# Six tile pairs of an MLP up projection as seven products of halves

## The chip, the cores and the metric

The program runs on one core of one Trainium2 chip. The metric is the device time of one execution in microseconds (us). Three timed runs of the kernel before gave 926.32, 927.02 and 927.61 us, with the median 927.02.

## The reference

One layer of a hybrid decoder, followed by a gated MLP, on 512 tokens (SEQ) of 1024 features (D_MODEL), in fp32. The mixers in front of the MLP stay as they are. What matters here is the MLP, whose hidden width D_FF is 3072, with a gate half and a value half:

```python
x = x + merged @ w_out[l]
h2 = rms_norm(x, norm_ffn[l])
up = causal_dwconv(h2 @ w_up[l], ffn_conv_w[l], ffn_conv_b[l])
gate_h, val_h = jnp.split(up, 2, axis=-1)
x = x + (jax.nn.gelu(gate_h, approximate=True) * val_h) @ w_down[l]
```

`w_up` is 1024 x 6144 and `w_down` 3072 x 1024. `causal_dwconv` has width 3: each output channel is a weighted sum of the same channel at a token and at the two tokens ahead of it, plus a bias. A root mean square norm with a gain ends the function.

## The kernel before

**Numbers.** TensorE works on fp32 data as two fp32r parts: `split` (L97, L98) rounds a tile to its high part on ScalarE and subtracts that from the tile on VectorE (or on GpSimd, where it is given as `eng`) for the low part. `mm3` (L104) makes a product from three passes, high by high, high by low and low by high, that add up in one PSUM bank. A product over 128 features is so three matmuls.

**The up projection.** The 3072 channels of each half are 24 tiles of 128. A *tile pair* is a gate tile and the value tile of the same channels. Normed x2 (`h2`, channels on partitions, tokens along the free axis) stays in SBUF as eight blocks of 128 features, high and low. One *unit* makes one tile: `fetch` (L166) loads a 128x1024 weight tile (512 KB) on SyncE's queue into one of three `raw` buffers, `split` makes its two parts, and `channel_major` issues 8 x 3 = 24 matmuls of 128x512 into one of five `mm` banks. `up_evac` then reads the bank: ScalarE scales by one convolution weight and adds the bias (L1162), and VectorE adds the two shifted terms in two steps (L1164). After the value tile `up_done` applies Gelu (L1174, ScalarE) and multiplies the halves (L1175, VectorE). The first three units are special: they multiply tokens 0 to 255 first and tokens 256 to 511 later, while the second half of the tokens is being normed and transposed (`norm2_flip`).

**Seven products.** The helper `seven`, used before this stage for two projections and after it for the first 20 tiles of the down projection (`down_fast`), makes a product of 2 x 2 blocks from seven block products rather than eight. Its blocks carry names: a1, a2, c1, c2, b1, b2, b3. Its weights are sums of blocks, and those are made in the transfer: a block is loaded by SyncE (L294), and then GpSimd issues transfers that add other blocks to the buffer where it lies (L299, *accumulating fetches*). A buffer to which a fetch adds must have been split before, since the sum replaces what was there.

**What sets the order.** The program is a list of *units*, which hold TensorE work, and *steps*. Each unit may name other work with a lead: `emit` places it that many units ahead (a weight tile is fetched and split two units ahead, AHEAD). `run` appends units and steps one after the other, and `blend` mixes the units of the up projection with those of `down_fast` evenly. The order of each engine's instructions comes from this list and a scheduler that has the tile dependencies. Each engine works through its own list in order, and an instruction that waits holds back those behind it. Activations, sums and fetched blocks share a pool of 51 slots of 128x512 fp32 (`fslot`, `rslot`). PSUM has five banks for `bank` and three for `sbank`.

At the end of the program `blend` runs tile pairs 12 to 19 with the down projection of tiles 0 to 11, and pairs 20 to 23 with that of tiles 12 to 19. Tile pairs 0 to 11 are run by themselves by `weave`, at about 537 to 656 us of the span: 24 units.

Of the kernel before, what the change touches and what calls it, by code (L numbers as in the profile page):

```python
# [8 lines left out]
F32 = mybir.dt.float32  # L9
# [4 lines left out]
AF = mybir.ActivationFunctionType  # L14
ALU = mybir.AluOpType
# [3 lines left out]
P = 128  # L19
# [38 lines left out]
def trunk(ctx: ExitStack, tc: tile.TileContext, x, xT, mem, memT, par, wdecay, wch, wv, wg, wmk,  # L58
# [20 lines left out]
    def rslot(shape=(P, S)):  # L79
        return apool.tile(list(shape), F32R, tag="s", name=nm("r"))  # L80
# [1021 lines left out]
    def down_units(wd, acts, after, between=None, left=None, nk=4):  # L1102

        def evac(t, ps, c):

            with tc.issue_after(queue.pop()) if queue else ExitStack():
                add = nc.vector.tensor_tensor(out=x2[t][c], in0=x2[t][c], in1=ps, op=ALU.add)
# [10 lines left out]
        lhs = lambda k, t: tuple(a[:, t * P:(t + 1) * P] for a in acts[k])  # L1118
# [32 lines left out]
    wo = down_units(wout, mr, norm2, norm2_flip)  # L1151
    step(lambda: residual(0))
    weave(wo[:4], [])
    step(lambda: residual(1))
# [15 lines left out]
    def up_done(ps, i, half, keep):  # L1170
        uph[half] = up_evac(ps, NF * half + i)
        if half:
            a, b = uph[0], uph[1]
            nc.scalar.activation(a, a, AF.Gelu_apprx_tanh)  # L1174
            nc.vector.tensor_tensor(out=a, in0=a, in1=b, op=ALU.mult)  # L1175
            keep(a)

    def up_units(tiles, keep, early=0):

# [19 lines left out]

    kept = {}

    def down_fast(at, np, acts, first, last):
# [3 lines left out]
        def sums(p):  # L1208

            A = {}  # L1210
            for j in range(2):
                ev, od = acts[2 * (2 * p + j)], acts[2 * (2 * p + j) + 1]
# [88 lines left out]
        else:  # L1301
            right()

    acts = [[] for _ in range(3)]

    def halves(a):
        r = (rslot(), rslot())
        split(*r, a)
        acts[2].append(r)
# [3 lines left out]
    blend(up_units(range(20, NF), halves), down_fast(3, 2, acts[1], False, True))  # L1313
    step(lambda: gain_rows(gfin))
    weave(down_units(wdown2, acts[2], final, None, final_left, 2), [])

    emit()

# [90 lines left out]
```

## Time and profile before

| | |
|---|---|
| median of three runs | 927.02 us |
| profiled execution | 928.05 us |
| its span, first to last instruction | 926.3 us |
| mean granted TensorE clock | 0.998 |
| busy: TensorE matmul, weight load | 99%, 84% |
| busy: VectorE, ScalarE, GpSimd | 68%, 54%, 12% |
| mean DMA rate | 126 GB/s |
| TensorE busy at 537 to 656 us (up projection alone) | 118.75 of 119.00 us |
| VectorE, ScalarE, GpSimd busy there | 65.93, 46.67, 0.00 us |
| DMA engines busy there | 0.28 |

Engines are PE (TensorE matmul), PEld (its weight load), DVE (VectorE), ACT (ScalarE), POOL (GpSimd) and SP (SyncE). L104 is line 104 of the kernel. In a list of single instructions the first two numbers are the start in the span and the duration in us, and brackets hold the idle time ahead and what ended it. In a group, `x48 | 37.5, 781 | 35.9` says 48 instructions, 37.5 us busy, 781 ns each, and 35.9 us of idle time ahead of them. In the table of stretches come the stretch and its length, then busy time (and instructions) of PE, PEld, DVE, ACT and POOL, then the granted clock, the busy share of the DMA engines and GB/s.

### The profile page before, as it was taken

Reading aid. Unit: us, or ns where it says so; the run is one execution under the profiler, and the core shown is the slowest. Engines: PE = TensorE matmul, PEld = TensorE weight load, DVE = VectorE, ACT = ScalarE, POOL = GpSimd, SP = SyncE. Lnnn points to the kernel's source line nnn. Section 1 sums busy time; section 2 is a strip of 40 time slices with the busy share of each in tenths; the row PEclk is TensorE's granted clock in tenths of the full one; section 3 lists DMA queues with packets and bytes.
Section 4 is the critical chain, followed back from the end, with each engine's and each line's share of the span. In section 5 each row is a group of like instructions: output and inputs, shape, how many; then the busy total and the mean of one; then the engine's idle time right before and its main releaser. Section 6 shows DMA issues by size and latency. Waiting matters only on the chain.

```text
span 926.3 us, 12066 instructions
## 1 busy us (share of the span) xinstructions
PE 914.6 (99%) x4390; PEld 776.4 (84%) x4390; DVE 631.8 (68%) x1104; ACT 498.1 (54%) x810; POOL 106.7 (12%) x144
## 2 busy tenths in 40 slices
PE   9999999999999999999999999999999999999996
PEld 7899888888889998888888798888888888888885
DVE  6997755665688567747776665555586666598765
ACT  6765655585855468484534334434445445445544
POOL 0010000000233430330000000000010140013102
PEclk9999999999999999999999999999999999999999
DMA  7446223213468783321157302234555594356622
GB/s 241 142 137 215 91 87 100 89 44 117 116 162 181 175 207 119 113 86 52 52 165 249 103 24 69 91 93 129 142 114 137 137 231 111 114 136 177 142 69 91
DMA packets 45994, 116.93 MB, mean 126 GB/s; under 512 B 5568, under 2 KB 13424, under 8 KB 45936
## 3 DMA queue, kind: packets, MB, share of 16 engines
q1 hardware_dynamic: 33920, 94.99, 31.9%
q0 software_dynamic: 11872, 20.92, 12.7%
q8 instruction: 34, 0.56, 0.2%
q10 hardware_dynamic: 144, 0.26, 0.1%
q14 instruction: 24, 0.20, 0.1%
HBM read 111.69 MB, written 3.67 MB: 125 GB/s over the span
## 4 chain that ended last, share of the span: by engine, by line
PE 86%; DVE 5%; DMA 4%; ACT 2%; issue 2%; SPq 0%; POOL 0%; DVEq 0%; ACTq 0%; POOLq 0%
PE mm L104 80%; DMA f<-in_wv 2%; PE mm L436 2%; PE sm L104 2%; DMA raw<-in_wup 2%; DVE wlo L98 2%; DVE r L98 1%; ACT r L97 1%; DVE f L392 0%; PE sm L996 0%; DMA raw<-in_wch 0%; ACT whi L97 0%; PE sm L983 0%; PE sm L1010 0%; DVE f L810 0%
## 5 line engine op out<-in xcount | busy, mean ns | idle before, releaser
L98 DVE TENSOR_TENSOR wlo<-raw,whi 128x1024 fp32r<-128x1024 f32 (+3 forms) x154 | 172.1, 1121 | 139.3 <-PE mm L104 71.6
L97 ACT ACTIVATE whi<-raw 128x1024 fp32r<-128x1024 f32 (+3 forms) x154 | 148.2, 968 | 173.6 <-PE mm L104 138.1
L104 PE MATMUL mm<-whi,r 128*128 128x512 f32 (+2 forms) x568 | 171.5, 372 | 0.0
L104 PE MATMUL mm<-h2l,whi 128*128 128x512 f32 x360 | 140.1, 389 | 0.0
L104 PE MATMUL mm<-h2h,whi 128*128 128x512 f32 x360 | 139.9, 389 | 0.0
L104 PEld LDWEIGHTS mm<-whi,r 128*128 128x128 f32 x568 | 105.6, 188 | 15.7 <-ACT r L97 0.3
L104 PE MATMUL mm<-hh,whi 128*128 128x512 f32 x288 | 113.4, 394 | 0.0
L104 PE MATMUL mm<-hl,whi 128*128 128x512 f32 x288 | 112.7, 391 | 0.0
L104 PE MATMUL mm<-wlo,r 128*128 128x512 f32 (+2 forms) x284 | 105.7, 372 | 0.5 <-DVE wlo L98 0.5
L104 PE MATMUL mm<-r,whi 128*128 128x512 f32 (+1 forms) x432 | 94.2, 367 | 0.0
L104 PE MATMUL mm<-h2h,wlo 128*128 128x512 f32 x360 | 88.9, 389 | 0.0
L104 PEld LDWEIGHTS mm<-r,whi 128*128 128x128 f32 x432 | 75.2, 189 | 13.1
L98 DVE TENSOR_TENSOR wlo<-f,whi 128x512 fp32r<-128x512 f32 (+2 forms) x90 | 53.7, 630 | 43.5 <-ACT whi L97 29.6
L299 POOL DMA_DIRECT2D f<-in_wdown x40 | 35.1, 1023 | 412.3 <-DMA f<-in_wdown 268.9
L97 ACT ACTIVATE whi<-f 128x512 fp32r<-128x512 f32 (+2 forms) x90 | 48.0, 579 | 59.9 <-PE mm L104 45.9
L104 PEld LDWEIGHTS mm<-h2h,wlo 128*128 128x128 f32 x360 | 67.6, 188 | 14.0
L104 PEld LDWEIGHTS mm<-h2l,whi 128*128 128x128 f32 x360 | 67.6, 188 | 14.0
L104 PEld LDWEIGHTS mm<-h2h,whi 128*128 128x128 f32 x360 | 67.5, 188 | 14.0
L1164 DVE SCALAR_TENSOR_TENSOR f<-mm,prm,f 128x511 f32<-128x511 f32 x96 | 71.4, 744 | 6.9 <-ACT f L1162 6.1
L104 PE MATMUL mm<-hh,wlo 128*128 128x512 f32 x288 | 71.4, 390 | 0.0
L104 PEld LDWEIGHTS mm<-hh,wlo 128*128 128x128 f32 x288 | 54.0, 188 | 11.2
L104 PEld LDWEIGHTS mm<-hh,whi 128*128 128x128 f32 x288 | 54.1, 188 | 10.8
(245 smaller groups left out, 1341.1 us busy)
## 6 DMA issues: line engine op xcount, KB each, us to landing
raw<-in_wup SPq DMA_DIRECT2D x48, 512.0 KB, 3.5
raw<-in_wch SPq DMA_DIRECT2D x39, 512.0 KB, 3.4
f<-in_wdown POOLq DMA_DIRECT2D x40, 256.0 KB, 5.9
raw<-in_wbr SPq DMA_DIRECT2D x24, 384.0 KB, 3.1
raw<-in_wdown SPq DMA_DIRECT2D x14, 512.0 KB, 3.5
f<-in_wdown SPq DMA_DIRECT2D x20, 256.0 KB, 4.4
raw<-in_wout SPq DMA_DIRECT2D x8, 512.0 KB, 3.6
f<-in_wv POOLq DMA_DIRECT2D x16, 200.0 KB, 5.7
```

The source lines that it names most:

```text
L97: nc.scalar.activation(hi, src, AF.Copy)
L98: return (eng or nc.vector).tensor_tensor(out=lo, in0=src, in1=hi.bitcast(F32), op=ALU.subtract)
L104: nc.tensor.matmul(ps, lhsT=l, rhs=r, start=first and i == 0, stop=last and i == len(seq) - 1, skip_group_check=more)
L299: nc.gpsimd.dma_start(raw[to, p][j], src(q, p)[:, j, :], accum_op=ALU.add)
L436: nc.tensor.matmul(ps[u], lhsT=w(a, u, k), rhs=xs["r"][k][j], start=k == 0 and i < n, stop=k == KD - 1 and i >= len(seq) - n)
L1164: nc.vector.scalar_tensor_tensor(out=a[:, j:], in0=ps[:, :S - j], scalar=col(C_FCW + 48 * (2 - j) + f), in1=a[:, j:], op0=ALU.mult, op1=AL ...
```

## The change

Six of the first twelve tile pairs (3, 4, 6, 7, 9 and 10) are made by `up_fast`, as seven products of halves; pairs 0, 1, 2, 5, 8 and 11 stay as they were. Gate and value tile make the two columns of the weight matrix (B11 and B21 the first and second 512 features of the gate tile, B12 and B22 those of the value tile), and the halves of the tokens make two rows of normed x2. Each of the seven products has 4 feature blocks of three matmuls each, 256 tokens wide: 12 matmuls of 128x256. a1, b1, b2 and b3 add up in one `mm` bank, c1 and c2 in one `sm` bank, a2 has another; after a1, c1, c2 and b3 ScalarE copies the bank to SBUF (L1263), and after a2, b1 and b2 VectorE adds or subtracts it. `up_evac` then works from SBUF, and `up_mix` is the old end of `up_done`.

The weight sums come from accumulating fetches (L1246): the buffer of B11 serves a1, then B12 is added for c1, then B22 for b1, then B21 for b3, and each split is followed by the fetch for the next use. B12 in a buffer of its own gets B22 added for b2. GpSimd makes the low parts of a2, c2 and b2. The sums of normed x2 (`h2_sums`) are sixteen GpSimd operations, eight for each half of the feature blocks, once for all six pairs; their splits are made with `h2_ready`. Each fast pair runs beside one ordinary unit: b1 of the pair before, a1, the unit, b2 of the pair before, c1, a2, b3 of the pair before, c2. `blend` starts with two units less, and the activations are kept in a dictionary by tile number rather than in three lists.

```diff
+    def h2_sums(p):
+        tt, f = nc.gpsimd.tensor_tensor, {}
+        for r in range(2):
+            for c in range(2):
+                at = slice(4 * c + 2 * p, 4 * c + 2 * p + 2), slice(r * HT, (r + 1) * HT)
+                f[r, c] = fslot((P, 2, HT))
+                tt(out=f[r, c], in0=h2["h"][(slice(None), *at)].bitcast(F32), in1=h2["l"][(slice(None), *at)].bitcast(F32),
+                   op=ALU.add)
+        tt(out=f[1, 1], in0=f[1, 0], in1=f[1, 1], op=ALU.subtract)
+        tt(out=f[1, 0], in0=f[0, 0], in1=f[1, 0], op=ALU.subtract)
+        tt(out=f[0, 0], in0=f[1, 1], in1=f[0, 0], op=ALU.subtract)
+        tt(out=f[0, 1], in0=f[0, 1], in1=f[0, 0], op=ALU.add)
...
+    def h2_ready(key, p):
+        f, h2s[key, p] = h2s[key, p], (rslot((P, 2, HT)), rslot((P, 2, HT)))
+        split(*h2s[key, p], f)
...
+    def up_fast(i, keep):
+
+        src = lambda q: wup[NF * (int(q[2]) - 1) + i][:, HB * (int(q[1]) - 1):HB * int(q[1])]
+        raw, w, st = {}, {}, {}
+
+        def load(q):
+            raw[q] = fslot()
+            loads.append(nc.sync.dma_start(raw[q], src(q)))
+
+        def ready(key, q, more=None):
+            w[key] = rslot(), rslot()
+            split(*w[key], raw[q], nc.gpsimd if key in ("a2", "c2", "b2") else None)
+            if more:
+                add(q, more)
+
+        def add(q, more):
+            nc.gpsimd.dma_start(raw[q], src(more), accum_op=ALU.add)
+
+        def run(key):
+            if key == "a1":
+                st["x"], st["o"] = bank((P, HT)), (fslot(), fslot())
+            elif key in ("a2", "c1"):
+                st[key] = sbank((P, HT))
+            ps = st["c1" if key[0] == "c" else "a2" if key == "a2" else "x"]
...
+            if key in ("a1", "c1", "c2", "b3"):
+                o = {"a1": g[:, one], "c1": v[:, two], "c2": v[:, one], "b3": g[:, two]}[key]
+                nc.scalar.activation(o, ps, AF.Copy)
+            elif key == "a2":
+                tt(out=g[:, one], in0=g[:, one], in1=ps, op=ALU.add)
+            else:
+                o = v[:, one if key == "b1" else two]
+                tt(out=o, in0=o, in1=ps, op=ALU.subtract)
+            if key == "b3":
+                up_mix(*(up_evac(a, NF * half + i) for half, a in enumerate((g, v))), i, keep)
+
+        pre = {
+            "a1": [(8, lambda: load("B11")), (3, lambda: ready("a1", "B11", "B12"))],
+            "a2": [(6, lambda: load("B21")), (3, lambda: ready("a2", "B21"))],
+            "c1": [(2, lambda: ready("c1", "B11", "B22"))],
+            "c2": [(6, lambda: load("B22")), (3, lambda: ready("c2", "B22"))],
+            "b1": [(2, lambda: ready("b1", "B11", "B21"))],
+            "b2": [(9, lambda: load("B12")), (6, lambda: add("B12", "B22")), (3, lambda: ready("b2", "B12"))],
+            "b3": [(2, lambda: ready("b3", "B11"))],
+        }
+        return {key: (p, lambda key=key: run(key)) for key, p in pre.items()}
...
-    weave(up_units(range(12), acts[0].append, 3), [])
-    blend(up_units(range(12, 20), acts[1].append), down_fast(0, 3, acts[0], True, False))
...
+    us = up_units((0, 1, 2, 5, 8, 11), whole, 3)
+    run(*us[:3], [lambda: h2_sums(0)], us[3], [lambda: h2_sums(1)], us[4], us[5],
+        [lambda k=k: h2_ready(k, 0) for k in ("c1", "c2", "b1", "b2")])
+
+    ahead = None
+    for i, u in zip((3, 4, 6, 7, 9, 10), us[6:]):
+        f = up_fast(i, whole)
+        run([ahead["b1"]] if ahead else [], [f["a1"]], u)
+        if not ahead:
+            run([lambda k=k: h2_ready(k, 1) for k in ("c1", "c2", "b1", "b2")])
+        run([ahead["b2"]] if ahead else [], [f["c1"], f["a2"]], [ahead["b3"]] if ahead else [], [f["c2"]])
+        ahead = f
+    us = up_units(range(12, 20), whole)
+    run([ahead["b1"]], us[0], [ahead["b2"]], us[1], [ahead["b3"]])
+    blend(us[2:], down_fast(0, 3, group(0), True, False))
```

**ScalarE at the first fast pair.** Before, in the middle of the up projection, ScalarE's list alternates bank read-outs (L1162), splits of whole weight tiles (`whi`) and a Gelu every second unit:

```order
L1162 ACTIVATE f_1078_5410<-mm_1077_5385,prm_76 128x512
L97 ACTIVATE whi_1090_5490<-raw_1089_5488 128x1024
L1162 ACTIVATE f_1083_5447<-mm_1082_5422,prm_76 128x512
L1174 ACTIVATE f_1083_5447<-f_1083_5447 128x512
L97 ACTIVATE whi_1095_5525<-raw_1094_5523 128x1024
L1162 ACTIVATE f_1088_5482<-mm_1087_5457,prm_76 128x512
```

In the changed program, the list in the first fast pair from the copy of a1 (`mm_1103_5474`) on; `f_1080_5371` to `f_1079_5369` are sums of normed x2 and `sm_1118_5540` is the bank of c1:

```order
L1263 ACTIVATE f_1104_5475<-mm_1103_5474 128x256
L97 ACTIVATE r_1106_5490<-f_1081_5377 128x512
L1162 ACTIVATE f_1109_5519<-mm_1108_5494,prm_76 128x512
L97 ACTIVATE r_1110_5523<-f_1080_5371 128x512
L97 ACTIVATE r_1112_5527<-f_1078_5367 128x512
L97 ACTIVATE r_1114_5531<-f_1077_5365 128x512
L1176 ACTIVATE f_1109_5519<-f_1109_5519 128x512
L97 ACTIVATE r_1116_5535<-f_1079_5369 128x512
L1263 ACTIVATE f_1105_5476<-sm_1118_5540 128x256
L97 ACTIVATE r_1119_5554<-f_1002_4860 128x512
```

The copy of c1, for which c2 waits since it adds to the same bank, now stands behind the ordinary unit's read-out, its Gelu and four splits of sums.

**GpSimd in the loop of the pairs.** Before, GpSimd's list has nothing for the up projection: it goes from clearing buffers in an earlier stage to the accumulating fetches of the down projection.

```order
L985 MEMSET f_793_3988 128x512
L985 MEMSET f_795_3996 128x512
L299 DMA f_1147_5889<-in_wdown 128x512
L299 DMA f_1148_5890<-in_wdown 128x512
L299 DMA f_1159_5965<-in_wdown 128x512
```

In the changed program, from the third fetch into the second pair's B11 buffer (`f_1082_5379`, for b3) to the first fetch into the fourth pair's (`f_1161_5801`); `f_1131_5618` is the third pair's, and `f_1169_5828` holds its sum for b2:

```order
L1246 DMA f_1082_5379<-in_wup 128x512
L1246 DMA f_1131_5618<-in_wup 128x512
L98 TENSOR_TENSOR r_1159_5783<-f_1139_5645,r_1158_5782 128x512
L98 TENSOR_TENSOR r_1168_5825<-f_1154_5761,r_1167_5824 128x512
L1246 DMA f_1131_5618<-in_wup 128x512
L1246 DMA f_1169_5828<-in_wup 128x512
L98 TENSOR_TENSOR r_1175_5877<-f_1160_5799,r_1174_5876 128x512
L1246 DMA f_1131_5618<-in_wup 128x512
L1246 DMA f_1161_5801<-in_wup 128x512
```

The fetches of two neighbouring pairs follow each other, with the subtractions of b2, a2 and c2 between them, and an issue that waits for a split holds back what stands behind it.

**SyncE's loads.** Before, SyncE's list in this stage has whole tiles only (`raw`, 512 KB). In the changed program a whole tile for the ordinary unit is followed by four blocks of 256 KB for fast pairs:

```order
L166 DMA raw_1287_6578<-in_wup 128x1024
L1237 DMA f_1154_5761<-in_wup 128x512
L1237 DMA f_1160_5799<-in_wup 128x512
L1237 DMA f_1161_5801<-in_wup 128x512
L1237 DMA f_1169_5828<-in_wup 128x512
L166 DMA raw_1302_6662<-in_wup 128x1024
```

The order tells that the four blocks stand behind the whole tile, not when they land.

More of the change, by code (lines that the diff above doesn't have):

```diff
@@ L1172, in up_done, with up_mix @@
         if half:
[L1173 to L1176, printed above, removed]
+            up_mix(uph[0], uph[1], i, keep)
+    def up_mix(a, b, i, keep):
+        nc.scalar.activation(a, a, AF.Gelu_apprx_tanh)
+        nc.vector.tensor_tensor(out=a, in0=a, in1=b, op=ALU.mult)
+        keep(i, a)
     def up_units(tiles, keep, early=0):
@@ L1302, in final, with whole, halves @@
             right()
[L1304 to L1309, printed above, removed]
-    weave(up_units(range(12), acts[0].append, 3), [])
-    blend(up_units(range(12, 20), acts[1].append), down_fast(0, 3, acts[0], True, False))
-    blend(up_units(range(20, NF), halves), down_fast(3, 2, acts[1], False, True))
+    acts = {}
+    def whole(i, a):
+        acts[i] = a
+    def halves(i, a):
+        acts[i] = rslot(), rslot()
+        split(*acts[i], a)
+    group = lambda first: lambda k: acts[first + k]
+    us = up_units((0, 1, 2, 5, 8, 11), whole, 3)
[12 more added lines that the diff above has]
+    blend(us[2:], down_fast(0, 3, group(0), True, False))
+    blend(up_units(range(20, NF), halves), down_fast(3, 2, group(12), False, True))
     step(lambda: gain_rows(gfin))
-    weave(down_units(wdown2, acts[2], final, None, final_left, 2), [])
+    weave(down_units(wdown2, group(20), final, None, final_left, 2), [])
     emit()
```

19 lines of the change are left out of this document (16 added, 3 removed).

## The prediction

> **What bounds the kernel now.** First the head of the page and its chain of waits, then the stretches of the up projection, then the order of time on ScalarE there.
>
> ```profile
> span 926.3 us, 12066 instructions
> PE 914.6 (99%) x4390; PEld 776.4 (84%) x4390; DVE 631.8 (68%) x1104; ACT 498.1 (54%) x810; POOL 106.7 (12%) x144
> PE 86%; DVE 5%; DMA 4%; ACT 2%; issue 2%; SPq 0%; POOL 0%; DVEq 0%; ACTq 0%; POOLq 0%
> core 0: us, PE busy (x) PEld busy (x) DVE busy (x) ACT busy (x) POOL busy (x), PEclk, DMA share, GB/s
> 560.00:575.00 15.00, 15.00 (x68) 12.43 (x67) 7.99 (x11) 6.68 (x8) 0.00 (x0) 1.00 0.20 70
> ```
> ```profile
> 568.32 0.78 ACT L1162 ACTIVATE f<-mm,prm 128x512 f32<-128x512 f32 x1 [0.75 <-PE mm L104]
> ...
> 571.95 1.06 ACT L97 ACTIVATE whi<-raw 128x1024 fp32r<-128x1024 f32 x1 [0.17 <-PE mm L104]
> 573.76 0.78 ACT L1162 ACTIVATE f<-mm,prm 128x512 f32<-128x512 f32 x1 [0.75 <-PE mm L104]
> ```
>
> TensorE is busy 99% of the span, and in the up stage it never pauses (15.00 of 15.00) while ScalarE waits for it before every read-out. So a removed matmul is worth its pitch, and any pause that the change brings is paid in full. The read-outs stand 5.44 us apart: one unit of 24 matmuls.
>
> **The products.** A busy time cannot price a matmul, since neighbours overlap. Starts can: two stretches of 24 in a row, 512 and 256 wide.
>
> ```profile
> 22.76 3.79 PE L104 MATMUL mm<-r,whi 128*128 128x512 f32 x16
> 26.39 1.98 PE L104 MATMUL mm<-r,wlo 128*128 128x512 f32 x8
> 28.20 3.79 PE L104 MATMUL mm<-r,whi 128*128 128x512 f32 x16
> ...
> 47.13 2.08 PE L104 MATMUL mm<-r,whi 128*128 128x256 f32 x16
> 49.05 1.12 PE L104 MATMUL mm<-r,wlo 128*128 128x256 f32 x8
> 50.01 2.08 PE L104 MATMUL mm<-r,whi 128*128 128x256 f32 x16
> ```
>
> 24 of 512 take 28.20 - 22.76 = 5.44 us (0.2267 each), 24 of 256 take 2.88 (0.120). Removed: 6 pairs x 2 tiles x 24 = 288 wide ones, 65.3 us. Added: 6 x 7 products x 12 = 504 half-wide ones, 60.5 us. So an eighth fewer columns gives **-4.8 us**, not an eighth of 65.3: 8.2 by columns, less 504 x 0.0067 for the narrower form.
> The Trainium skill, "TensorE: Matmul & The Clock Gate", section "Back-to-back issue gap", has N/2.4 + 2.5 ns: 215.8 and 109.2 ns. By it the sum would be 62.2 - 55.0, a gain of 7.1 us; the rows stand 11 ns above it at both widths, and they decide.
>
> **What the other engines get.** One fast pair and the ordinary unit beside it fill 84 x 0.120 + 5.44 = 15.5 us of TensorE.
>
> ```profile
> L97 ACT ACTIVATE r<-f 128x256 fp32r<-128x256 f32 x54 | 19.0, 405 | 0.0
> L97 ACT ACTIVATE r<-f 128x512 fp32r<-128x512 f32 x28 | 16.8, 620 | 3.3 <-DVE f L1175 3.3
> L1162 ACT ACTIVATE f<-mm,prm 128x512 f32<-128x512 f32 x48 | 37.5, 781 | 35.9 <-PE mm L104 35.9
> L1174 ACT ACTIVATE f<-f 128x512 f32<-128x512 f32 x24 | 15.0, 625 | 23.9 <-DVE f L1164 23.9
> ...
> L98 DVE TENSOR_TENSOR wlo<-raw,whi 128x1024 fp32r<-128x1024 f32 x106 | 131.2, 1238 | 117.4 <-PE mm L104 63.6 <-ACT whi L97 52.8 <-issue 0.8
> L1164 DVE SCALAR_TENSOR_TENSOR f<-mm,prm,f 128x510 f32<-128x510 f32 x48 | 35.7, 745 | 0.8
> L98 DVE TENSOR_TENSOR r<-f,r 128x256 fp32r<-128x256 f32 x54 | 21.5, 416 | 0.7 <-ACT r L97 0.7
> L98 DVE TENSOR_TENSOR r<-f,r 128x512 fp32r<-128x512 f32 x28 | 18.9, 684 | 0.8 <-ACT r L97 0.7
> ...
> L1275 POOL TENSOR_TENSOR f<-m,f 128x512 f32<-128x512 f32 x4 | 5.2, 1295 | 40.3 <-DVE m L1107 40.2
> ```
>
> ScalarE, by these means: 7 weight splits x 0.62, 4 bank copies x 0.41, 2 read-outs x 0.78, one Gelu 0.63, and 2.2 for the ordinary unit: 10.3 us. VectorE: 4 x 0.68, 3 x 0.42, 4 x 0.75, one product 0.69, 3.1 for the unit: 10.7 us. GpSimd: 3 subtractions x 1.30 = 3.9, and four issues of fetches, about one microsecond each by the rows further down. None reaches 15.5, so no engine becomes the bound: 0 us, under a cover of 4.8 us or more per pair. What can cost is order and latency.
>
> **First fast pair.** Product c2 adds into c1's bank and must wait for ScalarE's copy of c1. In ScalarE's list that copy stands behind a read-out, a Gelu that needs two VectorE steps, and splits of the sums. If the unit of tile 2 ends at 573.6 (its read-out row above), a1 ends at 575.0, the ordinary unit at 580.5, c1 and a2 (24 matmuls) at 583.4. ScalarE: about 0.7 left over from earlier splits, read-out 0.78, then VectorE 0.75 + 0.68 + 0.75, Gelu 0.63, split 0.62, copy 0.41: 5.3 us, so 585.8 and with handovers 585.9. TensorE waits **+2.5 us**, once. Ends: 1.7 without that backlog, 3.8 with one GpSimd operation (1.30) in VectorE's way. Later pairs have 2.9 us of other products between c1 and c2, and no such Gelu in front.
>
> **The chain of the fetches.** All of a1, c1, b1, b3 share one buffer, into which three fetches add; ScalarE splits a1 of the next pair only after b1 of this one. So the pairs hang together in a loop: b1 split, add, c1 split, add, next b1 split. The landings:
>
> ```profile
> L299 POOL DMA_DIRECT2D f<-in_wdown x1: 921/921/921, 662.1 to 662.1; - x1
> DMA to landing us min/median/max: 4.1/4.1/4.1
> ...
> L299 POOL DMA_DIRECT2D f<-in_wdown x2: 857/1000/1142, 672.7 to 673.3; - x2
> DMA to landing us min/median/max: 4.1/4.8/5.5
> ...
> L299 POOL DMA_DIRECT2D f<-in_wdown x1: 863/863/863, 757.0 to 757.0; - x1
> DMA to landing us min/median/max: 6.0/6.0/6.0
> ```
> ```profile
> 662.00:667.00 5.00, 5.00 (x24) 4.14 (x23) 4.78 (x10) 1.82 (x2) 1.80 (x2) 1.00 0.35 52
> 672.00:678.00 6.00, 6.00 (x28) 4.99 (x27) 6.00 (x14) 3.02 (x6) 1.75 (x2) 1.00 0.54 85
> 757.00:764.00 7.00, 7.00 (x33) 5.79 (x32) 6.40 (x10) 2.52 (x4) 3.79 (x6) 1.00 0.98 240
> ```
>
> One alone lands after 4.1 us where DMA is 0.35 busy, and the leading one of two after 4.1 at 0.54, but one after 6.0 at 0.98; of two issued together the second lands at 673.3 + 5.5, that is 6.1 after the first issue. An issue holds GpSimd for 0.86 to 1.14, and how the two elementwise engines meet is seen once in the trace, around 385 to 390 (VectorE, then GpSimd):
>
> ```profile
> 384.75 0.67 DVE L963 TENSOR_TENSOR f<-f,f 96x512 f32<-96x512 f32 x1
> ...
> 387.66 1.21 DVE L98 TENSOR_TENSOR wlo<-raw,whi 128x1024 fp32r<-128x1024 f32 x1
> ...
> 389.40 1.78 DVE L963 TENSOR_TENSOR f<-f,f 96x512 f32<-96x512 f32 x1
> ```
> ```profile
> 385.50 2.22 POOL L965 TENSOR_TENSOR f<-f,f 96x512 f32<-96x512 f32 x1 [1.90 <-DVE f L963]
> 387.69 2.94 POOL L966 TENSOR_TENSOR f<-f,f 96x512 f32<-96x512 f32 x1
> ```
>
> The loop, from the landing before b1: split 0.62 + 0.68; b3's add goes out, the next pair's first add behind it lands 6.1 later; splits of c1 and a2 1.24, GpSimd's subtraction for a2 1.30, which stands before the next issue; then a landing of 4.1 to 6.0; and some 0.6 for six handovers (estimate, 0.1 each, from the 0.08 between VectorE's end at 385.42 and GpSimd's start at 385.50 in these rows). That is 10.5 plus the last landing: 14.6 to 16.5 us against the 15.5 of TensorE.
> How much the first step has to spare: the second pair's a1 starts at 585.9 + 2.9 (c2 and b1 of the first) = 588.8, and its b1 14.1 later at 602.9, so its fetch has to land by 602.2. a1 of that pair is split by 587.5, its first add lands near 593.1, and the second goes out 2.7 us later, at 595.9: it may take 6.3 us.
> Just then SyncE, released by the split of an ordinary unit, sends 512 KB and three or four loads of 256 KB in a burst. So I take 5.5 for this landing, nearer to the busy row: a loop of 16.0, 0.55 late at each of four steps (second to sixth pair), less 0.7 spare: **+1.5 us**. Ends: 0 (landing 4.1) and 3.9 (landing 6.0: four steps of 1.05, spare 0.3).
>
> **The sums of normed x2.** Sixteen GpSimd operations that the trace does not have.
>
> ```profile
> 548.46 1.29 DVE L98 TENSOR_TENSOR h2l<-sm,h2h 128x512 fp32r<-128x512 f32 x2 [1.99 <-ACT h2h L97]
> ...
> 560.10 0.74 DVE L1164 SCALAR_TENSOR_TENSOR f<-mm,prm,f 128x510 f32<-128x510 f32 x1
> ```
>
> Six of the first eight start when normed x2 is whole (549.8); then comes an accumulating fetch that waits for the first weight split on VectorE (560.84 + 0.68 = 561.5); the other eight end at 561.5 + 0.87 + 8 x 1.30 = 572.8, wanted at 581.9. Cost 0; the cover is 9 us.
>
> **The rest.** The loads and splits of the ordinary units stand further ahead than before: 0. Loads for the down projection come later, with over a unit (5.44) in hand: 0; without that cover one landing, 4 to 6 us, would show. Its stage keeps 21 products and loses two up units of cover, 14 for 16: 0.
>
> **Sum.** -4.8 + 2.5 + 1.5 = -0.8 us. The profiled execution took 928.05 us (span 926.3 and 1.75 around it) and would take 927.25; the three runs shown have the median 927.02, 1.0 lower, and I forecast 927.02 - 0.8 = 926.2. About 0.2%, 1.9 us, is what a measurement can tell from no change.
>
> **Rivals.** (1) *The loop stays hidden.* Adds land in 4 to 5 us, as at 662 and 672; only the first pair's wait is left: -2.3, or -3.1 with its short end: about 924.5. For it: the landing at 672 kept 4.1 with VectorE busy without a pause (6.00 of 6.00) and DMA half busy. Against: the burst. Chance 0.35.
> (2) *The loop rules, slower.* A b1 that waits in every pair takes the place of the columns saved. From a last landing of 5.0 us the loop exceeds 15.5; at 5.7 its steps have eaten the 2.3 us that the first pair leaves, at 6.1 the kernel is slower by 0.2%. GpSimd's subtraction sits in it too, and can be blocked, as the rows of 384 to 390 show. Begun while VectorE subtracted, GpSimd's took 2.94 instead of 1.30, and VectorE's next subtraction-like step 1.78 instead of 0.67: they take turns. With a quarter of that 1.64 (0.4) and a landing of 6.0 the loop is 16.95: four steps of 1.45 and 0.1 already in the first, 5.9; -4.8 + 2.5 + 5.9 = +3.6, about 930.6. Against: where that subtraction falls, VectorE has only c1's split and mostly waits for ScalarE. Chance 0.24.
> The Trainium skill, "SBUF — State Buffer", section "SBUF: two separate sides", calls the pair of ports that both engines share an exclusive lock held for the whole instruction. By that rule each of GpSimd's operations waits out one of VectorE's; the two rows agree.
> (3) *The change does not shorten TensorE's work*, because each half-wide matmul takes as long as its weight load:
>
> ```profile
> L104 PEld LDWEIGHTS mm<-whi,r 128*128 128x128 f32 x568 | 105.6, 188 | 15.7 <-ACT r L97 0.3
> ```
>
> 504 x 0.188 = 94.8 instead of 65.3 us: +29.5, 956.5. Against: the 256-wide rows at 47.13 had a load for each and kept 0.120, so loads overlap. Chance 0.02.
>
> **How the numbers follow.** Forecast 0.39, rival (1) 0.35, (2) 0.24, (3) 0.02. So faster by over 0.2% 0.35, within 0.39, slower 0.26. The range goes from the saving with 1.0 of waits (923.2) (a first pair in which VectorE's steps are done early) to rival 2's price (930.6); outside lie a loop blocked more than a quarter and rival (3). The forecast's own range, inside 0.2%, is 925.2 to 928.8.
>
> **What would show it.** Right: TensorE waits in the first fast pair for ScalarE's copy, some 2.5 us, and in the later pairs for ScalarE's split of b1, growing from none to under 1 us a pair; 24 half-wide matmuls in 2.88 us. Wrong: no wait at b1 (rival 1), waits of 1 to 2 us at every b1, with GpSimd operations near 3 us (rival 2), or waits at other products, which my chain leaves out: then its step from landing to landing is wrong.

## The result, and the profile after

The changed kernel takes 935.65 us (median of four runs, 935.00 to 935.83), the kernel before 926.89 us beside it (926.32 to 927.61): a ratio of 1.0093, 95% interval 1.0075 to 1.0110, or 8.8 us slower. The forecast was 926.2 us with a range up to 930.6. The head of the page after and its chain of waits:

```profile
span 934.1 us, 12758 instructions
PE 916.4 (98%) x4606; PEld 785.9 (84%) x4606; DVE 660.1 (71%) x1142; ACT 518.3 (55%) x872; POOL 174.3 (19%) x202
PE 79%; DVE 9%; DMA 5%; issue 3%; ACT 2%; POOL 0%; SPq 0%; POOLq 0%; ACTq 0%; DVEq 0%
```

TensorE was meant to be busy some 5 us less, and is busy 1.8 us more (914.6 before); on the chain of waits its share falls from 86% to 79% and VectorE's rises from 5% to 9%. Where that happens is seen in stretches of 5 us around the first fast pair:

```profile
core 0: us, PE busy (x) PEld busy (x) DVE busy (x) ACT busy (x) POOL busy (x), PEclk, DMA share, GB/s
575.00:580.00 5.00, 5.00 (x24) 4.03 (x22) 3.29 (x6) 4.69 (x8) 0.74 (x1) 1.00 0.69 176
580.00:585.00 5.00, 2.15 (x14) 1.53 (x12) 5.00 (x9) 4.64 (x9) 1.63 (x2) 1.00 0.23 85
585.00:590.00 5.00, 3.04 (x13) 2.53 (x14) 5.00 (x6) 1.90 (x4) 1.75 (x2) 0.63 0.95 294
590.00:595.00 5.00, 5.00 (x31) 5.00 (x31) 1.81 (x4) 1.58 (x4) 3.08 (x3) 0.69 0.60 137
595.00:600.00 5.00, 5.00 (x27) 4.24 (x26) 0.69 (x1) 2.07 (x4) 1.63 (x2) 1.00 0.26 42
```

From 580 to 590 TensorE is busy for only 5.2 of 10 us while VectorE has no pause, and then two stretches show a granted clock of 0.63 and 0.69. In the order of time on TensorE there:

```profile
581.68 0.39 PE L104 MATMUL sm<-h2h,r 128*128 128x256 f32 x1 [0.73 <-ACT r L97]
...
585.57 0.74 PE L104 MATMUL sm<-h2h,r 128*128 128x256 f32 x4 [2.69 <-POOL r L98]
...
587.36 1.86 PE L104 MATMUL sm<-r,r 128*128 128x256 f32 x7 [0.92 <-DVE r L98]
589.69 2.93 PE L104 MATMUL sm<-r,r 128*128 128x256 f32 x12 [0.47 <-ACT f L1263]
```

Four waits, 4.81 us: a2 for its high and then for its low part (GpSimd), the second half of c1 for the low part of a sum (VectorE), and only last, with 0.47 us, c2 for the copy of c1 that the prediction had named. And c2's twelve matmuls span 2.73 us (589.69 to the next product at 592.42) where twelve took 1.44 in the prediction's rows: half the clock. In the stretch from 587 to 593 TensorE is busy 5.17 us at a granted clock of 0.50, so 2.6 us went there, with the edges about 2.8. From the start of a1 of the first pair to a1 of the second are 20.9 us (573.24 to 594.17), by its products 12.64: **8.3 us lost** in one pair, 4.8 in waits, 2.8 by the clock, the rest in the slow restart after four waits.

Why VectorE was late stands in its order of time, and beside it in GpSimd's:

```profile
562.84 5.64 DVE L98 TENSOR_TENSOR wlo<-raw,whi 128x1024 fp32r<-128x1024 f32 x1 [1.72 <-ACT whi L97]
...
569.95 1.59 DVE L1177 TENSOR_TENSOR f<-f,f 128x512 f32<-128x512 f32 x1
571.47 2.30 DVE L98 TENSOR_TENSOR wlo<-raw,whi 128x1024 fp32r<-128x1024 f32 x1
```
```profile
562.05 5.33 POOL L1212 TENSOR_TENSOR f<-h2h,h2l 128x512 f32<-128x512 f32 x4
567.46 2.17 POOL L1214 TENSOR_TENSOR f<-f,f 128x512 f32<-128x512 f32 x1
...
583.37 0.86 POOL L1246 DMA_DIRECT2D f<-in_wup  x1 [7.62 <-DVE r L98]
583.93 2.82 POOL L98 TENSOR_TENSOR r<-f,r 128x512 fp32r<-128x512 f32 x2
```

A subtraction that takes 1.23 us elsewhere takes 5.64 next to the sums of normed x2, since it waits out four of GpSimd's operations; with the next two, VectorE is 6.4 us behind. Then GpSimd itself waits 7.62 us for one of VectorE's low parts before it may issue a fetch, and a2's low part stands behind that.

The later pairs run nearly as forecast. The last four matmuls of a1 in the second and third pair, and the one wait between the a1 of the fourth and of the fifth, in b3 of the third:

```profile
595.13 0.64 PE L104 MATMUL mm<-h2h,r 128*128 128x256 f32 x4
...
610.67 0.64 PE L104 MATMUL mm<-h2h,r 128*128 128x256 f32 x4
...
637.92 0.74 PE L104 MATMUL mm<-h2h,r 128*128 128x256 f32 x4 [0.25 <-DVE r L98]
```

The a1 rows are 15.54 us apart, as the 15.5 of the prediction. The interval from the third to the fourth pair is 15.54 too, the next two are 16.12, and 0.4 us more go in the last pair: 1.5 us lost in all. The last loss is at the entry of the down projection; SyncE, ScalarE and TensorE:

```profile
680.87 2.37 SPq L294 DMA_DIRECT2D f<-in_wdown  x4
```
```profile
688.35 1.25 ACT L97 ACTIVATE whi<-f 128x512 fp32r<-128x512 f32 x2 [5.29 <-DMA f<-in_wdown]
```
```profile
694.81 0.50 PE L104 MATMUL mm<-whi,r 128*128 128x512 f32 x1 [1.00 <-DVE r L98]
695.81 0.73 PE L104 MATMUL mm<-whi,r 128*128 128x512 f32 x2 [0.49 <-DVE r L98]
```

Of six blocks of down weights that the kernel before loads at 641 to 658 us, two are issued at 666 us here and four at 681, when the pool has slots again (SyncE waited 11.8 us for products to release them). In the median of the six they land 7.5 us later; ScalarE's split waits 5.29 us and holds back the read-outs behind it, VectorE gets the end of the last pairs and the sums for the first down products at once, and TensorE waits four times. Counted from start to start, these cost 3.0 us: the first twelve matmuls of 512 columns take 4.78 us (692.73 to 697.51) where twelve take 2.72, the next twenty-four 6.42 (702.95 to 709.37) where they take 5.44.

The account of the two spans (926.3 and 934.1): -4.8 for the products, +8.3 first pair, +1.5 later pairs, +3.0 entry, and 0.3 that the run after was ahead when a1 began (573.24 against 573.56): 7.7 of 7.8 us.

That 0.3 hides one more loss. At 538 us the run after was 1.6 us ahead (it lacks a pause of 0.45 us that the kernel before has at 526, and was 0.7 ahead before that). Then come the first two additions of the sums, on GpSimd, VectorE and TensorE:

```profile
534.04 2.55 POOL L1212 TENSOR_TENSOR f<-h2h,h2l 128x512 f32<-128x512 f32 x2 [117.23 <-DVE st L116]
```
```profile
534.54 0.81 DVE L117 TENSOR_TENSOR st<-st,st 128x1 f32<-128x1 f32 x1
535.39 1.22 DVE L118 SCALAR_TENSOR_TENSOR st<-st,st 128x1 f32<-128x1 f32 x1
```
```profile
545.08 0.74 PE L104 MATMUL mm<-h2h,r 128*128 128x256 f32 x4 [0.31 <-DVE r L98]
546.28 0.74 PE L104 MATMUL mm<-h2h,r 128*128 128x256 f32 x4 [0.46 <-DVE r L98]
```

Two small steps of the norm, 0.16 us each elsewhere, take 0.81 and 1.22, and TensorE pays later: from 537.99 to 548.15 are 10.16 us, where the same work takes 8.87 in the kernel before (539.61 to 548.48) and with the sums left out (538.45 to 547.32). So the sums cost 1.3 us before the first pair begins, too.

### The profile page after: what moved, and what is told of

The parts are those of the page before. It is cut to its first block, busy times and chain, and to the rows that moved or that the text cites. A ratio compares the mean times of both kernels' runs of the same rounds, so it can differ in the third digit from the quotient of the medians.

```text
span 934.1 us, 12758 instructions
## 1 busy us (share of the span) xinstructions
PE 916.4 (98%) x4606; PEld 785.9 (84%) x4606; DVE 660.1 (71%) x1142; ACT 518.3 (55%) x872; POOL 174.3 (19%) x202
## 3 DMA queue, kind: packets, MB, share of 16 engines
q0 software_dynamic: 15328, 27.21, 16.9%
## 4 chain that ended last, share of the span: by engine, by line
PE 79%; DVE 9%; DMA 5%; issue 3%; ACT 2%; POOL 0%; SPq 0%; POOLq 0%; ACTq 0%; DVEq 0%
PE mm L104 71%; DMA f<-in_wup 3%; PE sm L104 3%; DVE wlo L98 2%; PE mm L436 2%; DVE r L98 2%; DMA raw<-in_wup 2%; DVE f L1164 1%; DMA f<-in_wdown 1%; ACT r L97 1%; ACT whi L97 0%; DVE f L1129 0%; PE sm L211 0%; DVE f L392 0%; PE sm L996 0%
## 5 line engine op out<-in xcount | busy, mean ns | idle before, releaser
L98 DVE TENSOR_TENSOR wlo<-raw,whi 128x1024 fp32r<-128x1024 f32 (+3 forms) x142 | 163.6, 1156 | 86.7 <-ACT whi L97 42.6
L97 ACT ACTIVATE whi<-raw 128x1024 fp32r<-128x1024 f32 (+3 forms) x142 | 135.6, 960 | 138.7 <-PE mm L104 107.4
L104 PE MATMUL mm<-h2l,whi 128*128 128x512 f32 x264 | 102.8, 390 | 0.0
L104 PE MATMUL mm<-h2h,whi 128*128 128x512 f32 x264 | 102.7, 390 | 0.0
L98 DVE TENSOR_TENSOR r<-f,r 128x512 fp32r<-128x512 f32 (+3 forms) x126 | 73.0, 601 | 20.4 <-ACT r L97 20.0
L97 ACT ACTIVATE r<-f 128x512 fp32r<-128x512 f32 (+3 forms) x144 | 70.1, 534 | 30.1 <-DMA f<-in_wup 25.5
L104 PE MATMUL mm<-r,r 128*128 128x512 f32 (+2 forms) x336 | 65.5, 346 | 0.0
L104 PE MATMUL mm<-h2h,wlo 128*128 128x512 f32 x264 | 65.2, 389 | 0.0
L104 PEld LDWEIGHTS mm<-hl,whi 128*128 128x128 f32 x288 | 54.1, 188 | 10.7
```

What stands on the lines that cost most here:

```text
L97: nc.scalar.activation(hi, src, AF.Copy)
L98: return (eng or nc.vector).tensor_tensor(out=lo, in0=src, in1=hi.bitcast(F32), op=ALU.subtract)
L104: nc.tensor.matmul(ps, lhsT=l, rhs=r, start=first and i == 0, stop=last and i == len(seq) - 1, skip_group_check=more)
```

## The experiments

The kernel before was timed beside each set of versions; its medians are 926.89 to 927.47 us. "First pair" is the time from the start of a1 of the first pair to that of the second, 12.64 us by its products. It, and what is lost at the entry, is read from the profiled execution, which doesn't always lie at the median.

### One cause at a time

**The sums left out.**

```diff
-        tt, f = nc.gpsimd.tensor_tensor, {}
...
+        for key, r, c in (("c1", 1, 1), ("b2", 1, 0), ("b1", 0, 0), ("c2", 0, 1)):
+            at = slice(4 * c + 2 * p, 4 * c + 2 * p + 2), slice(r * HT, (r + 1) * HT)
+            h2s[key, p] = h2["h"][(slice(None), *at)].bitcast(F32)
```

> The changed kernel with the sixteen GpSimd sums left out: the splits read the high parts of normed x2 instead (so the fast pairs' values are wrong). Theory A (GpSimd's second eight sums hold VectorE; its split of a weight tile took 5.64 us there instead of 1.23, and the first fast pair lost 8.3 us with the fall of the clock that followed the pause): the first pair loses at most the 2.5 us of the bank copy, VectorE's splits there stay at 1.2 us, the granted clock stays at 1.00; 928.0 to 930.0 us. Theory B (GpSimd's own order: the subtraction for a2 stands behind a fetch that waits for c1's split, whoever made the sums): the wait for GpSimd of 2.7 us and the fall of the clock stay; 933.5 us or more. Theory C (entry of the down projection, 2.8 us of pauses there) is left as it is in both.

932.83 us against 927.05, ratio 1.0065 (1.0048 to 1.0082). Both theories missed: 2.8 us came back (in the trace 0.8 ahead of the first pair, 1.0 in it and about 1.1 in the later ones), but the first pair still takes 19.9 us, with the clock at 0.50. VectorE is not behind at 579 us any more, and then this happens, on VectorE, GpSimd and TensorE:

```profile
579.56 4.04 DVE L98 TENSOR_TENSOR wlo<-raw,whi 128x1024 fp32r<-128x1024 f32 x1 [0.75 <-ACT f L1254]
```
```profile
579.67 2.84 POOL L98 TENSOR_TENSOR r<-f,r 128x512 fp32r<-128x512 f32 x2
```
```profile
584.91 1.48 PE L104 MATMUL sm<-r,r 128*128 128x256 f32 x7 [2.72 <-DVE r L98]
```

GpSimd's two low parts, for a2 and c2, now fall on a weight split of VectorE, which takes 4.04 instead of 1.23 us, and the low part behind it is what TensorE waits for.

**The low parts on VectorE, the sums as they were.**

```diff
-            split(*w[key], raw[q], nc.gpsimd if key in ("a2", "c2", "b2") else None)
+            split(*w[key], raw[q])
```

> The changed kernel with the low parts of a2, c2 and b2 on VectorE instead of GpSimd; the sums stay on GpSimd. Theory A: VectorE is behind by some 6 us when the first fast pair begins, and gets 0.68 us more per part, so the wait moves from GpSimd to VectorE and stays, with the fall of the clock: 934 to 937 us. Theory B: the 2.7 us of the wait for GpSimd go, and with a pause of 2 us or less the clock stays up: 929 to 931 us.

933.18 us against 927.05, 1.0062 (1.0047 to 1.0077). Theory A's mechanism held for the first pair, though its 934 us or more did not: the wait moved to VectorE (3.5 us in two waits) and stayed, 20.6 us with the clock at 0.50. The gain comes from places neither theory spoke of: in the trace no wait is left at the entry of the down projection, and the later pairs stand 15.54 us apart. That trace is of the fastest execution of four (931.05 us, the others 932.85 to 933.64), so part of this is not shown for the others.

**The sums on VectorE.**

```diff
-        tt, f = nc.gpsimd.tensor_tensor, {}
+        tt, f = nc.vector.tensor_tensor, {}
```

> The changed kernel with the sixteen sums on VectorE (16 x 0.68 = 10.9 us more work there, nothing that blocks it). Theory A: VectorE has some 10 us idle between 549 and 575 us, so most of the sums fit, it is at most 2 us behind at the first fast pair instead of 6; 928 to 931 us. Theory B: as before the move, 933.5 us or more. A third possibility, that the amount of work and not the block is what puts VectorE behind: 934 to 937 us, with VectorE busy without a pause from 560 to 590 us.

936.26 us against 927.05, 1.0099 (1.0084 to 1.0114): the third possibility. VectorE is busy 4.96, 5.00, 4.75 and 5.00 us in the four stretches of 5 us from 560 to 580, and the first pair takes 23.0 us. So 10.9 us of plain work there do as much harm as 6.4 us of blocking: what counts is that VectorE is late at 580 us, not what made it late.

**The clock by itself.** The kernel before, with five pauses.

```diff
+    PAUSES = {7: 0, 11: 2, 15: 3, 19: 4, 22: 6}
...
+    def pause(ps, m):
+        r = rslot()
+        nc.scalar.activation(r, ps, AF.Copy)
+        for _ in range(m):
+            nc.scalar.activation(r, r.bitcast(F32), AF.Copy)
+        held.append(r)
...
+        nc.tensor.matmul(ps, lhsT=r[:, :P], rhs=r, start=True, stop=False, skip_group_check=True)
```

> The kernel before with five pauses of TensorE put into the up projection, 4 units apart: after the 8th, 12th, 16th, 20th and 23rd unit the next one begins with a matmul that waits for a chain of 1, 3, 4, 5 and 7 ScalarE copies (so one product too many is added to five tiles). Lengths about 1.2, 2.8, 3.4, 3.9 and 4.9 us, 16 us in all. If the loss of 3.5 us beyond the pauses in the first fast pair is the clock's answer to a pause: behind the longer ones the granted clock falls to 0.5 for some 6 us, which costs up to 3.3 us each, and behind the short ones it doesn't; three falls give about 953 us. If the clock there fell for another reason (half-wide matmuls, a load of all engines): it stays at 1.00 and the time is about 943 us.

950.22 us in one run, beside 927.05. The second and third pause on TensorE, and stretches around both:

```profile
609.11 0.50 PE L1190 MATMUL mm<-r 128*128 128x512 f32 x1 [2.54 <-ACT r L1185]
...
634.60 0.50 PE L1190 MATMUL mm<-r 128*128 128x512 f32 x1 [3.20 <-ACT r L1185]
```
```profile
607.00:612.00 5.00, 2.89 (x13) 2.39 (x14) 3.09 (x4) 2.03 (x4) 0.00 (x0) 1.00 0.33 108
633.00:638.00 5.00, 3.40 (x9) 2.69 (x10) 1.92 (x3) 1.48 (x3) 0.00 (x0) 0.70 0.34 105
```

Pauses of 0.69 and 2.54 us left the clock alone, and those of 3.20, 3.86 and 5.56 us brought it to 0.50 for a few us. The five sum to 15.85 us, the added matmuls to 1.1, and 950.22 - 927.05 is 23.2: about 6.2 us for three falls, some 2 each, from one execution. So a pause alone brings the clock down in a kernel that has no half-wide matmuls here, and the later pairs have these without a fall (twelve in 1.44 us): the 2.8 us of the first pair follow its pauses.

### Causes together

**Sums left out and low parts on VectorE** (both edits above).

> The changed kernel with both of GpSimd's shares gone: the sixteen sums left out (the fast pairs' values are wrong) and the low parts of a2, c2 and b2 on VectorE. Each alone left a pause of 3.8 to 4.7 us in the first fast pair and the clock fell. Theory A2 (two blocks of VectorE, either of them enough: the sums cost it 6.4 us, the two low parts held a weight split for 2.8 us in the run without sums): now no split on VectorE takes longer than 1.3 us there, the only pause left is c2's wait for the copy of c1, 0.5 to 2.5 us, the clock stays at 1.00, and the entry of the down projection is without a pause as in the run with the low parts on VectorE; 927.05 - 0.3 - 4.8 + 1.2 + (0.5 to 2.5) = 923.6 to 925.6 us. Rival B2 (the chain of fetch, split and fetch is late in the first pair whatever GpSimd does): a pause over 3 us and the fall of the clock stay, 929 us or more.

928.36 us against 927.24, 1.0011 (1.0002 to 1.0019). With no elementwise work on GpSimd the first pair still takes 19.0 us: waits of 0.55 and 1.66 us for VectorE's low parts and 1.07 for the copy of c1, 3.3 in all, and the clock fell again. A2 was incomplete. Splits of VectorE there take 0.68 and 1.23 us, as elsewhere; it simply has twenty operations between 574.5 and 588.6 us. Eight of them, and eight of ScalarE's activations, are the splits of the sums, once for all six pairs, in front of and within the first. The wait of 1.66 us is c1's for one of them (583.28 us): in VectorE's list it stands behind the adding of a2's bank, which waits for a2's matmuls, and a read-out step.

**And c2 in a bank of its own.**

```diff
-            elif key in ("a2", "c1"):
+            elif key in ("a2", "c1", "c2"):
...
+            if key == "c2":
+                tt(out=v[:, one], in0=v[:, two], in1=ps, op=ALU.add)
```

> As the run without sums and with the low parts on VectorE, and c2 in a bank of its own, added to the copy of c1 on VectorE instead of in the bank. Theory A2: the wait of c2 goes, no pause over 0.5 us is left in the first fast pair: 922.5 to 924 us, which is the saving of 4.8 us less some 1 us in later pairs. If c1's copy is not what c2 waits for (rival: its own weights or sums end last), the time is that of the run before within 0.5 us. Rival B2: 929 us or more.

928.82 us against 927.24, 1.0020 (1.0010 to 1.0029). The first pair falls to 15.8 us, since its waits (0.55, 1.05, 0.16 and 0.33) sum to 2.1 us and not 3.3, and the clock no longer falls: 1.2 us by the waits, 2.1 by the clock. The total didn't move, because the entry's pauses are back (2.6 us from start to start). By its time alone, within 0.5 us of the run before, this would be the rival; the two profiles tell that a gain in one place was lost in another. Why the pauses came back is open.

**The sum splits ahead of the first pair** (in addition).

```diff
-    run(*us[:3], [lambda: h2_sums(0)], us[3], [lambda: h2_sums(1)], us[4], us[5],
-        [lambda k=k: h2_ready(k, 0) for k in ("c1", "c2", "b1", "b2")])
+    run(*us[:3], [lambda: h2_sums(0), lambda: h2_sums(1)], us[3], us[4],
+        [lambda k=k: h2_ready(k, 0) for k in ("c1", "c2", "b1", "b2")], us[5],
+        [lambda k=k: h2_ready(k, 1) for k in ("c1", "c2", "b1", "b2")])
```

> As the run without sums, with the low parts on VectorE and c2 in its own bank, which still lost 3.1 us in the first fast pair (waits of 0.55, 1.05, 0.16 and 0.33 us, mostly for VectorE's low parts); now all eight splits of the (left out) sums stand ahead of the first pair, four of them after the fifth unit and four after the sixth. Theory A3 (besides GpSimd's two blocks, eight splits of sums for all pairs are queued on ScalarE and VectorE just where the first pair's own weights are split): the first pair loses under 1 us; 926.0 to 927.0 us, with the pauses of the entry left (2.6 us). Rival (what is late there is the chain of fetches, not the amount of splits): as before, 928 to 929 us.

926.87 us against 927.47, 0.9998 (0.9988 to 1.0007). A3 holds, with 14.3 us for the first pair; it loses 1.6 us, not under 1, with one wait of 1.19 us for the split of b1. At the entry, after waits of 1.17 and 0.50 us, the clock fell (0.57 in the stretch from 688 to 692 us). The profiled execution took 928.42 us, though, 1.6 more than the median, and whether the others had that fall is not shown.

### The sums earlier

Adds of the first half of the tokens at once, the other twelve operations in one piece, low parts on VectorE; then also c2 in its own bank.

```diff
+    def h2_rows(r):
+        for p in range(2):
+            for c in range(2):
...
+    run([lambda: h2_rows(0)], *us[:3], [lambda: h2_rows(1), lambda: h2_sums(0), lambda: h2_sums(1)], *us[3:6],
```

> The changed kernel with the right sums made earlier: GpSimd adds the high and low parts of the first half of the tokens as soon as they are there (about 541 us), does the other twelve operations in one piece from 549 to 565 us, ahead of the first accumulating fetch, and VectorE makes the low parts of a2, c2 and b2. Theory A2: a weight split of VectorE at 562 us is held for some 2 to 3 us instead of 6.4, and it has caught up by 577 us; 924 to 927 us, without a fall of the clock. If the sums cost as much there as later (the same 16 operations block VectorE, wherever they stand): 931 to 933.5 us, as with the low parts alone on VectorE.

> As the run with early sums and the low parts on VectorE, and c2 in a bank of its own. Theory A2: 923 to 925 us, the first version with right values that is faster than the kernel before. If the copy of c1 ends nothing: as the run with early sums, within 0.5 us. If the sums' block is as dear as before: 930 to 933 us.

934.04 us, 1.0072 (1.0059 to 1.0085), and 932.69 us, 1.0054 (1.0041 to 1.0067), against 927.24. Theory A2's times were missed in both. The first pairs take 19.0 and 15.8 us, just as without any sums (19.0 and 15.8): here the sums cost the pair nothing. They cost ahead of it: TensorE waits 1.41 us at 541 us for the norm of the last tokens and 1.47 at 549 for a low part, and a1 of the first pair starts 3.9 us later than without sums (576.40 against 572.46). VectorE and GpSimd at that place:

```profile
537.69 1.22 DVE L116 TENSOR_TENSOR st<-st 128x1 f32<-128x1 f32 x1
538.95 1.20 DVE L117 TENSOR_TENSOR st<-st,st 128x1 f32<-128x1 f32 x1
540.19 0.16 DVE L118 SCALAR_TENSOR_TENSOR st<-st,st 128x1 f32<-128x1 f32 x1
```
```profile
535.11 5.02 POOL L1213 TENSOR_TENSOR f<-h2h,h2l 128x512 f32<-128x512 f32 x4 [117.69 <-DVE st L116]
```

Operations on one element per partition, 0.16 us each, take 1.2 while GpSimd adds: each waits out one of its operations, whatever its own size. A chain of small steps pays at every step. The changed kernel lost its 1.3 us at this place in the same way, with two additions where here there are four.

### The entry, and everything together

**Three units ahead of the first down product** (alone, on the changed kernel).

```diff
-    run([ahead["b1"]], us[0], [ahead["b2"]], us[1], [ahead["b3"]])
-    blend(us[2:], down_fast(0, 3, group(0), True, False))
+    run([ahead["b1"]], us[0], [ahead["b2"]], us[1], [ahead["b3"]], us[2])
+    blend(us[3:], down_fast(0, 3, group(0), True, False))
```

> The changed kernel with three units of the up projection, not two, ahead of the first down product. Theory C (the entry's 2.8 us of pauses come from loads of down weights that wait for slots of the pool and land 5.3 us late for ScalarE's queue; one unit of 5.44 us covers them): no pause at the entry, 932.5 to 933.5 us. Rival (the loads wait for the same products, so they move with them): 935 to 936 us. Theories A2 and A3 say nothing here: the first pair keeps its 8.3 us.

932.99 us, 1.0056 (1.0042 to 1.0070): 2.7 us less than the change, and from 660 to 760 us TensorE has no wait. Theory C holds: with the loads at hand the 3.0 us of the entry are gone.

**All causes taken away, the sums kept**: ScalarE copies the fp32 halves from the transposes' banks, so that GpSimd has eight operations left; the low parts, the bank, the splits and the entry as above.

```diff
+                nc.scalar.activation(hf[p, t // 2, g][:, :, t % 2 * P:(t % 2 + 1) * P], pt[:, 2 * p:2 * p + 2, :], AF.Copy)
```

> A version with right values that takes away every cause found: the fp32 halves of normed x2 are copied by ScalarE from the transposes' banks (sixteen copies of 128x256), so GpSimd has eight operations and not sixteen, done by 561 us before VectorE's weight splits; low parts on VectorE; c2 in its own bank; sum splits ahead of the first pair; three units ahead of the first down product. Theory (GpSimd's blocks, the bulge of splits, the bank's copy, the clock and the entry are all of the loss): the saving of 4.8 us less 1 to 2 us, 923.5 to 925 us. If something else holds the pairs back (the loop of fetches, the half-wide matmuls): 927 us or more.

924.21 us (923.53 to 924.61) against 927.47, 0.9961 (0.9949 to 0.9974): faster than the kernel before, and 11.4 us faster than the change. The head of its page, and the one wait left in the pairs:

```profile
span 922.5 us, 12727 instructions
PE 910.9 (99%) x4606; PEld 783.9 (85%) x4606; DVE 654.7 (71%) x1166; ACT 522.4 (57%) x882; POOL 137.9 (15%) x176
```
```profile
585.16 1.70 PE L104 MATMUL mm<-r,r 128*128 128x256 f32 x12 [1.22 <-ACT r L97]
```

TensorE is busy 3.7 us less than before. The saving of 4.8 less the 1.7 us of the first pair (14.3 us) is 3.1; measured were 3.3. That the two agree so well is in part luck: the spans of the two profiled executions differ by 3.8 us, and 1.2 of these were gained before a1 of the first pair (572.38 against 573.56), since the pause at 526 us is missing there too. What follows gained 2.6.

**The same with the low parts of a2, c2 and b2 on GpSimd.**

> As the version before it, with the low parts of a2, c2 and b2 on GpSimd as in the change. Theory A2 (GpSimd's operations hold VectorE's): two operations in the first pair hold a weight split by up to 2.8 us, with a pause of 0 to 2.5 us that does not reach the length at which the clock fell (between 2.5 and 3.2 us), and the later pairs lose 0.5 us more in all: 924.5 to 927.5 us. If offloading is worth what it frees (VectorE is the late engine): faster than the version before it by 0.5 us or more.

929.39 us, 1.0017 (1.0008 to 1.0026): 5.2 us slower than without, more than expected, so the offloading costs more than it frees. TensorE's waits between 560 and 720 us:

```profile
PE mm L104 <- DVE f L1269: 2.6, 3, 1.0
PE mm L104 <- ACT r L97: 1.6, 1, 1.6
PE mm L104 <- DVE r L98: 0.5, 2, 0.3
```

In the later pairs b3, which adds to the bank of b2, waits for VectorE's subtraction (L1269), and that stands behind a weight split that takes 1.50 us on average from 600 to 660, against 1.23 in the version without. The intervals of the pairs grow from 15.54 to 16.9 and 17.2 us there. This puts the low parts back on GpSimd by themselves; the sums and the splits of sums were not put back by themselves.

| kernel | us | first pair, us | lost at the entry, us |
|---|---|---|---|
| the change | 935.65 | 20.9 | 3.0 |
| no sums | 932.83 | 19.9 | 3.2 |
| low parts on VectorE | 933.18 | 20.6 | 0 |
| sums on VectorE | 936.26 | 23.0 | 2.3 |
| no sums, low parts on VectorE | 928.36 | 19.0 | 0 |
| and c2's own bank | 928.82 | 15.8 | 2.6 |
| and splits ahead | 926.87 | 14.3 | 4, with the clock |
| entry alone | 932.99 | 20.7 | 0 |
| all, sums kept | 924.21 | 14.3 | 0 |
| all, low parts on GpSimd | 929.39 | 15.9 | 0 |

## Why the prediction was wrong, point by point

**The products: right.** Twelve half-wide matmuls take 1.44 us, a pair and its unit 15.54 us, as worked out; the version without most of the other losses is 3.3 us faster than the kernel before, which fits a saving near 4.8.

**"None reaches 15.5, so no engine becomes the bound: 0 us": failed for the first pair.** The sum was made for an average pair. The first one also carries eight splits of sums for all pairs (8 x 0.62 us on ScalarE, 8 x 0.68 on VectorE). Where GpSimd did nothing elementwise, waits of 3.3 us were left in the pair; with c2 in its own bank they were 2.1, and with these splits moved ahead too 1.2.

**"The sums of normed x2. Cost 0; the cover is 9 us": failed.** They ended at 574.9 us, near the 572.8 forecast, and were in time for their own users. But the step asked only when they are ready and not whom they hold up. The rows of 384 to 390 in the prediction showed GpSimd and VectorE taking turns, and rival (2) priced it for one subtraction; for the sixteen sums it was not priced. They held the norm's small steps, for 1.3 us ahead of the first pair, and put VectorE 6.4 us behind just before it. That is the step at fault, though not alone: without the sums the low parts on GpSimd took their place, and without both the bulge of splits with the shared bank did; after each the clock fell. Low parts on GpSimd were enough for a fall in the profiled execution of the last version (after 1.57 us), the bulge and the shared bank were enough without GpSimd; that the sums are enough without the bulge is not shown. So taking one of them away shortened the pair by 1.0 us at most (20.9 to 19.9), and all of them and the bank by 6.6 of its 8.3.
By the Trainium skill, "SBUF — State Buffer", section "Who interferes with whom", a VectorE instruction with two SBUF inputs contends with a GpSimd one that reads SBUF, and what they contend for is an exclusive lock. The trace agrees, and adds that a wait can be longer than one instruction (5.64 us beside four in a row).

**First pair, +2.5 us for the copy of c1: the place was there, the size was not the pair's.** The copy cost 0.47 us after the other waits, and 1.07 when those were smaller.

**The clock: left out.** A pause was "paid in full"; it was paid more than in full, 2.8 us on 4.8. The profile before shows nothing of it in this stage, where TensorE never pauses for longer than 0.25 us.

**The loop, +1.5 us: right in size by luck, wrong in place.** Fetches landed after 5.7 us in the median (3.8 to 8.1), where 5.5 was taken, and the later pairs lost 1.5 us. But the waits are in b3, for VectorE's low part, not at b1 for ScalarE's split. Rival (2), with its price of 930.6, was wrong: the slower result did not come from the loop.

**"Loads for the down projection come later, with over a unit in hand: 0": failed**, +3.0 us. The step named its own price without cover, one landing, and the landing was longer (7.5 us). What it missed is the pool: the loads waited for slots, and there was no unit in hand.

Open: which length of pause, or what share of a stretch, brings the clock down. The five single pauses gave a bound between 2.54 and 3.20 us, but in the last version it fell after one of 1.57 us, without sums and low parts after waits of 0.55, 1.66 and 1.07 us close together, and with the splits ahead after 1.17 and 0.50; a wait of 1.22 us left it alone.

## What to carry to other kernels

Work moved to an idle engine is free only when it shares nothing with the busy ones: for each operation on GpSimd with SBUF inputs, look at what VectorE does in the same microseconds, small operations above all. Work that is done once for a loop should be summed with the first pass of the loop and not averaged over it. And where several causes each suffice for a pause, taking them away one by one shows little; take all away, and then put them back one by one.

## What the runs showed of the hardware

After pauses of TensorE of 3.20 us and more the granted clock went to 0.50 for some us, at about 2 us a time in the run with pauses. The Trainium skill, "TensorE: Matmul & The Clock Gate", section "HAM oscillation — how this bites in real kernels", asks for no idle gap over about 3.4 us: the pauses of 2.54 (no fall) and 3.20 (fall) are near that, though the fall comes below it, and the fall after 1.57 us is far below.

VectorE's operations with two inputs in SBUF wait for GpSimd's whatever their size (0.16 us became 1.2 on one element per partition), while those with one input in PSUM, such as the convolution's steps, kept theirs (two in 1.52 us at 568.40, beside a sum of GpSimd).
